# A two-layer streaming encoder on one core: weight low parts on VectorE, x1 and x3 held whole, z's gain moved to its rows, later turns and norm

## The chip, the core and the metric

The kernel runs on one core of a Trainium2 chip. The metric is device time in microseconds (us). Before the change the kernel took 2825.17 us, the median of 3 runs (2823.48 to 2830.65). A program of the core sends work to five engines, each with its own queue served in order: TensorE (PE; weight loads are shown apart as PEld), VectorE (DVE), ScalarE (ACT), GpSimd (POOL) and SyncE (SP), which issues the transfers.

## The reference, cut to what matters

Sequence 2048, width 1024, 16 heads of 64, all in float32. Layer 0 is a causal pooling mixer, layer 1 is stick-breaking attention; each is followed by a gated embedding.

```python
def rms_norm(x, g):
    return x * rsqrt(mean(x * x, axis=-1) + EPS) * g

def pool_mixer(h, w_in, w_group, scale, w_out):
    u, z = split(h @ w_in, 2)
    # four channel groups: trailing means over 2, 4, 8, 16 frames, minus the frame
    mixed = einsum('bsgc,gcd->bsgd', pooled(u), w_group) * scale
    return (mixed * silu(z)) @ w_out

# layer 0
x = x + pool_mixer(rms_norm(x, a_norm), a_w_in, a_w_group, a_scale, a_w_out)
x = x + (p[0] @ ple_w[0]) * sigmoid(x @ ple_gate_w[0])
# layer 1
k, v = split(rms_norm(x, kv_norm) @ w_kv, 2)
q, z = split(rms_norm(x, b_norm) @ b_w_in, 2)
k, q = rms_norm(heads(k), k_norm), rms_norm(heads(q), b_q_norm)
# strictly causal, beta = sigmoid(q.k / 8), blocks of 128 queries
o = sum over s < t of beta[t,s] * prod(1 - beta[t,j], s < j < t) * v[s]
x = x + (o * silu(z)) @ b_w_out
x = x + (p[1] @ ple_w[1]) * sigmoid(x @ ple_gate_w[1])
```

In the kernel's words x1 is the stream after the mixer's residual, x2 the stream after layer 0, x3 the stream after the attention's residual.

## The kernel before

**Layout.** The stream is held transposed: 8 tiles of 128 channels, in 4 chunks of 512 tokens, so a tile is 128x512. Every float32 operand of a product is split in two tiles, a high part (`F32R`, a cast of the value, on ScalarE) and a low part (value minus high part), and a product is three matmuls: high by high, high by low, low by high. `split` (L188, L189) does this for activations, with the low part on the engine that its caller names; `put_split` does it for weights.

**Weights.** `plan` lists all weight units in the order in which they are used; `pump` loads them ahead into 9 buffers (`wpair`), and `take` and `give_back` move along that list. A unit's raw tile lies in `io`, a ring of 4 buffers that other loads use too. For weights without a gain (a norm's factor per input channel), ScalarE casts the high part (L208, kept in program order), and a counter `lo` decides who makes the low part (L210): in the first stage (boot) VectorE, then two of three on GpSimd and the third on VectorE. For weights with a gain, ScalarE multiplies by it (L214) and VectorE does the low part (L215), twice for a unit, once for each of its halves.

**Stages.** The program is one long list of steps, one for each matmul, and what is to happen some steps later is put off by `after`, `late` and `store`.

1. Opening (solo: no attention runs). Chunk 0's mixer and `gated_part(0)`, chunk 1's mixer and `gated_part(1)`. Side work is drawn in steps: `prep` loads, splits and squares the next chunk's x; `mixtures` makes combined weights for the job (in `mx` tiles); `prefill` scales chunk 0's x2 rows for it.
2. `pair_part(0, 1)`, the first *job*: v, k and q of two chunks by a scheme of seven products (p1 to p7) on half-width blocks in place of eight. The PSUM tiles are `total` and `own`. Row sets: p1 and p2 come from `prefill`, the others from `build`, whose first four steps make p5, p7, p3 and p6 and the next four p4. It ends with `reload`, which loads the first chunk's x2 rows, scales them by the norm (L844) and splits them on GpSimd, for z.
3. Attention for the queries of chunks 0 and 1 (48 slots, each a head and a chunk of keys), with `beside_first` drawn beside it: z of chunks 0 and 1, chunk 2's mixer and gate, chunk 3's mixer. VectorE runs the scans of the attention (L1126) and the low parts of `at` (L1146) there.
4. `middle`: `gated_part(3)` and `pair_part(2, 3)`, the second job.
5. Attention for chunks 2 and 3 (112 slots), beside z of chunks 2 and 3 and the output part `post` of chunks 0 to 2; then `post(3)` alone.

**x1 and x3.** `out_steps` adds the residual into the loaded tile `xr` (in `io`), splits the sum into a pair and keeps only the pair. `gate_steps` needs the sum again, and rebuilds it on GpSimd as `xj`, high plus low (L702, 64 times).

**Norms and turns.** `norm2` puts two tasks in a list, `lag`: the sum of squares over channels (`pst<-ones,acc`, after 24 steps) and the broadcast of the factors (`pst<-ident,r`, after 48 steps, giving `rb2`, whose tile is `rby`). For k and q, `keyed` normalises per head (L751) and puts four turns (`finish`, `pst<-ident,qs`) in the list 44 steps later: TensorE turns the tile, ScalarE copies it, GpSimd makes the low part (`hl`, L765), SyncE stores. `timed` takes one task at a time, at least 9 steps apart, as they fall due. Before each job `settled_lag` runs all tasks that are left at once, and `pair_part` runs `build`'s first four steps ahead of the first product:

```python
        side = build(c1)
        for _ in range(4):
            next(side)
        back = reload(c0)
        for n, _ in enumerate(job(c0, c1)):
            if n >= 120 and n % 10 == 0:
                next(side, None)
            if n >= total - 58 and n % 6 == 0:
                next(back, None)
```

`tmp` has 6 buffers, `row` 11, `pair` 17, `pp` 8. `row` holds the squares' sum of `prep` (`acc`), two of `prep`'s last splits (`xh`, `xl`) and the raw rows of `prefill`.

## Time and profile before

The profiled execution took 2824.62 us and its span, from the first to the last instruction, is 2822.8 us. The granted clock of TensorE was 0.975 over the span.

| stage (us of the span) | length | PE | DVE | ACT | POOL | clock |
|---|---|---|---|---|---|---|
| boot, chunk 0's mixer (0 to 140) | 140 | 136.02 | 100.48 | 71.78 | 42.53 | 1.00 |
| `gated_part(0)` and around it (140 to 260) | 120 | 99.14 | 58.05 | 61.28 | 92.17 | 0.97 |
| chunk 1's mixer, `gated_part(1)` (260 to 444) | 184 | 184.00 | 91.79 | 50.59 | 90.81 | 1.00 |
| first job (444 to 726) | 282 | 254.30 | 169.92 | 147.08 | 219.91 | 0.94 |
| first attention (726 to 1405) | 679 | 651.63 | 508.43 | 393.71 | 313.77 | 0.98 |
| `gated_part(3)` (1405 to 1450) | 45 | 38.12 | 27.17 | 19.80 | 31.44 | 0.93 |
| second job (1450 to 1749) | 299 | 257.47 | 166.82 | 146.53 | 231.19 | 0.91 |
| second attention (1749 to 2718) | 969 | 950.39 | 857.58 | 571.89 | 134.73 | 0.99 |
| `post(3)` (2718 to 2823) | 105 | 100.07 | 23.09 | 14.49 | 18.90 | 1.00 |

How to read it: the columns are busy times in us, the last is the clock that TensorE was granted. The difference between length and PE is what TensorE waited in that stage; it is largest in the first gated stage and in the two jobs, where GpSimd is at its fullest. Busy matmuls are not all at full speed: a clock below 1 means that some of them ran slower.

### The profile page before, as it was taken

What the parts mean: (1) busy time and instruction counts of PE and PEld (TensorE: products, weight loads), DVE (VectorE), ACT (ScalarE), POOL (GpSimd) and SP (SyncE); (2) the same over time, 40 slices, a digit from 0 to 9 for tenths busy, and PEclk for the clock granted to TensorE, in tenths of its full rate; (3) what the DMA queues carried; (4) which work ended last, traced back from release to release, by engine and by line L of the source; (5) the groups of instructions that cost most, each with busy time, mean ns of one, the idle gap of its engine ahead of it and who ended that gap; (6) DMA issues with size and microseconds to landing.
All of it is one profiled execution on the core that took longest, in us unless ns stands there. A gap on an engine that the chain in (4) does not pass through costs nothing.

```text
span 2822.8 us, 38660 instructions
## 1 busy us (share of the span) xinstructions
PE 2671.1 (95%) x13118; PEld 2216.6 (79%) x13118; DVE 2003.3 (71%) x2523; ACT 1477.2 (52%) x2922; POOL 1175.4 (42%) x889
## 2 busy tenths in 40 slices
PE   9988997999799998999989997999999999999999
PEld 7866886878588887888867775888888878887887
DVE  6744736465767877788574545888999888899942
ACT  5453233465676546555444564666655655555531
POOL 1468455787654426642466788100111011111111
PEclk9999998999899999999989998999999999999999
DMA  7898544856899765766448676775665556556454
GB/s 256 313 385 311 203 164 131 285 174 207 297 382 317 266 233 193 280 220 239 146 130 246 202 216 198 245 243 180 205 216 179 182 175 222 183 170 223 158 197 162
DMA packets 315362, 630.77 MB, mean 223 GB/s; under 512 B 47646, under 2 KB 80414, under 8 KB 315164
## 3 DMA queue, kind: packets, MB, share of 16 engines
q1 hardware_dynamic: 314588, 627.51, 66.6%
q8 instruction: 104, 1.70, 0.3%
q10 hardware_dynamic: 576, 0.79, 0.1%
q14 instruction: 94, 0.77, 0.1%
HBM read 463.03 MB, written 165.15 MB: 223 GB/s over the span
## 4 chain that ended last, share of the span: by engine, by line
PE 40%; DVE 9%; POOL 5%; DMA 3%; issue 3%; ACT 2%; SPq 0%; POOLq 0%; ACTq 0%; DVEq 0%
PE psd L51 19%; PE pso L51 7%; PE psl L51 6%; PE psa L55 6%; DVE pp L1126 3%; DVE at L1146 2%; PE own L51 1%; POOL wpair L210 1%; PE total L51 1%; POOL xs L189 1%; DMA wraw<-in_gate_a_dram 1%; POOL rq L181 1%; DVE sg L713 1%; POOL hl L765 1%; DMA xw<-x2d 0%
## 5 line engine op out<-in xcount | busy, mean ns | idle before, releaser
L1126 DVE TENSOR_TENSOR_SCAN pp<-pp,floor 128x512 f32<-128x512 f32 (+3 forms) x640 | 748.4, 1206 | 8.1 <-ACT pp L1122 8.0
L51 PE MATMUL psd<-x,wpair 128*128 128x512 f32 x2304 | 575.6, 395 | 28.8 <-POOL wpair L210 10.1
L51 PEld LDWEIGHTS psd<-x,wpair 128*128 128x128 f32 x2304 | 432.3, 190 | 126.3 <-POOL wpair L210 13.1
L1144 ACT CAST at<-psa 128x512 fp32r<-128x512 f32 (+3 forms) x640 | 303.5, 526 | 394.9 <-PE psa L55 393.4
L1146 DVE TENSOR_TENSOR at<-psa,at 128x512 fp32r<-128x512 f32 (+3 forms) x640 | 359.8, 601 | 139.4 <-ACT at L1144 137.8
L51 PE MATMUL pso<-at,vv 128*128 128x512 f32 (+3 forms) x1280 | 322.6, 369 | 29.5 <-DVE at L1146 23.9
L1122 ACT ACTIVATE pp<-psl 128x512 f32<-128x512 f32 (+3 forms) x640 | 312.3, 548 | 10.5 <-PE psl L51 9.9
L51 PE MATMUL psd<-xp,wpair 128*128 128x512 f32 x1248 | 303.4, 392 | 0.4 <-DVE wpair L215 0.2
L51 PEld LDWEIGHTS pso<-at,vv 128*128 128x128 f32 x1280 | 230.1, 189 | 93.5 <-DVE at L1146 42.9
L51 PE MATMUL total<-wpair,xs 128*128 128x512 f32 x1152 | 289.4, 408 | 11.8 <-POOL wpair L210 8.8
L55 PE MATMUL psa<-ident,pp 128*128 128x128 f32 x2176 | 293.7, 275 | 0.0
L55 PEld LDWEIGHTS psa<-ident,pp 128*128 128x128 f32 x2176 | 254.4, 141 | 28.1 <-issue 0.4
L51 PEld LDWEIGHTS total<-wpair,xs 128*128 128x128 f32 x1152 | 223.0, 197 | 62.0 <-POOL wpair L210 11.2
L51 PEld LDWEIGHTS psd<-xp,wpair 128*128 128x128 f32 x1248 | 231.8, 188 | 50.6 <-DVE wpair L215 1.3
L51 PE MATMUL psl<-kk,qa 128*128 128x512 f32 (+3 forms) x640 | 259.3, 410 | 0.0
L1169 POOL TENSOR_TENSOR os<-os,zt 128x512 f32<-128x512 f32 x32 | 52.1, 1629 | 488.4 <-ACT os L1168 482.8
L51 PE MATMUL psl<-kk,qb 128*128 128x512 f32 (+3 forms) x640 | 234.8, 367 | 3.4 <-ACT qb L1089 3.4
L51 PE MATMUL own<-wpair,xs 128*128 128x512 f32 x864 | 212.7, 403 | 19.4 <-ACT wpair L208 10.2
L210 POOL TENSOR_TENSOR wpair<-wraw,wpair 128x512 fp32r<-128x512 f32 x128 | 180.7, 1420 | 93.6 <-ACT wpair L208 82.8
L51 PEld LDWEIGHTS own<-wpair,xs 128*128 128x128 f32 x864 | 165.4, 194 | 57.2 <-POOL wpair L210 11.4
L702 POOL TENSOR_TENSOR xj<-x 128x512 f32<-128x512 f32 x64 | 105.5, 1653 | 202.5 <-DMA out_dram<-sg 100.9
L51 PE MATMUL psd<-og,wpair 128*128 128x512 f32 x744 | 184.5, 390 | 0.0
(144 smaller groups left out, 4042.7 us busy)
## 6 DMA issues: line engine op xcount, KB each, us to landing
wpair<-once SPq DMA_DIRECT2D x288, 512.0 KB, 4.5
kk<-kd SPq DMA_DIRECT2D x160, 256.0 KB, 3.4
vv<-vd SPq DMA_DIRECT2D x160, 256.0 KB, 3.4
once<-wpair SPq DMA_DIRECT2D x48, 512.0 KB, 6.1
wpair<-wf SPq DMA_DIRECT2D x48, 512.0 KB, 5.7
xw<-x2d SPq DMA_DIRECT2D x72, 256.0 KB, 4.5
once<-kp SPq DMA_DIRECT2D x36, 512.0 KB, 4.9
wraw<-in_gate_a_dram SPq DMA_DIRECT2D x64, 256.0 KB, 3.2
```

The costliest lines, as they stand in the source:

```text
L51: return held_in_order(nc.tensor.matmul(*a, **k))
L55: return held_in_order(nc.tensor.transpose(*a, **k))
L181: G.tensor_tensor(out=out_ap, in0=ms, in1=neghalf[:, 0:w], op=ALU.pow)
L189: low = lambda: lo.tensor_tensor(out=half_of(pr, 1), in0=src, in1=f(half_of(pr, 0)), op=ALU.subtract)
L210: (G if state["lo"] % 3 and not state["boot"] else V).tensor_tensor(out=pr[:, 1], in0=raw, in1=f(pr[:, 0]), op=ALU.subtract)
L702: G.tensor_tensor(out=xj, in0=f(x1[o][:, 0]), in1=f(x1[o][:, 1]), op=ALU.add)
L713: V.tensor_tensor(out=sg, in0=sg, in1=xj, op=ALU.add)
L1122: A.activation(out=pp[:, r0:], in_=ps[:, :w], func=AF.Sigmoid, scale=-1.0)
L1126: V.tensor_tensor_scan(out=pp[:, r0:][:, ::-1], data0=pp[:, r0:][:, ::-1], data1=least, initial=1.0 if st["diag"] else st["carry"][j], op0 ...
L1144: A.copy(out=at[:, 0, cs], in_=pt[:, cs])
L1146: return lambda: V.tensor_tensor(out=at[:, 1, cs], in0=pt[:, cs], in1=f(at[:, 0, cs]), op=ALU.subtract)
L1169: G.tensor_tensor(out=os, in0=os, in1=zt, op=ALU.mult)
```

## The change

- `put_split`: the low part of a weight without gain is on VectorE while no attention runs, and beside attention for every second weight; the others stay on GpSimd.
- `plan_z`: the weights of z are loaded without gain, so they are split by the line above; `reload` gets the gain `g_b` and multiplies it into the rows in the same pass as the norm's factors. Its raw rows now lie in `tmp` in place of `io`.
- `out_steps` can write the sum to a tile of its own in `row` (`x1`) and keep it; `gate_steps` then uses it, and nothing is rebuilt. This is done for chunks 0 and 2 of layer 0 and for all four chunks of layer 1: 48 of 64 rebuilds go. `prep` needs one `row` pair less, and takes a pair of `act` in its place.
- The turns of k and q come 60 steps after their rows in place of 44, the norm's sums after 30 in place of 24.
- `settled_lag` goes: the tasks left over fall due inside the job, and `build`'s first four steps run at the job's first step at which `rb2` is there.

```diff
@@ -207,7 +207,7 @@
         if gain is None:
             held_split(A.copy(out=pr[:, 0], in_=raw))
             state["lo"] += 1
-            (G if state["lo"] % 3 and not state["boot"] else V).tensor_tensor(out=pr[:, 1], in0=raw, in1=f(pr[:, 0]), op=ALU.subtract)
+            (V if state["solo"] or state["lo"] % 2 else G).tensor_tensor(out=pr[:, 1], in0=raw, in1=f(pr[:, 0]), op=ALU.subtract)
             return
         for i, kt in enumerate(kts):
             g = gain[:, kt : kt + 1]
@@ -311,7 +311,7 @@
 
     def plan_z():
         for b in range(4):
-            plan_block("zb", b_w_z, b, g_b, True)
+            plan_block("zb", b_w_z, b, None, True)
 
     plan_a(0)
     first_chunk = len(plan)
@@ -527,7 +527,7 @@
         for o in range(KT):
             xin = io("xin")
             nc.sync.dma_start(out=xin, in_=x[o * P : (o + 1) * P, s * W5 : (s + 1) * W5])
-            pr = pair("xp") if o < 6 else (row("xh", F32R), row("xl", F32R))
+            pr = pair("xp") if o < 7 else (row("xh", F32R), row("xl", F32R))
             split(pr, xin, G)
             ck["x"].append(pr)
             gather_squares(ck, "acc1", o, xin)
@@ -639,7 +639,7 @@
 
 
 
-    def out_steps(acts, residual, ahead=lambda: None):
+    def out_steps(acts, residual, ahead=lambda: None, whole=None):
         res, requested = [], deque()
 
         def request(o):
@@ -665,9 +665,13 @@
                 request(2 * b + k + 2)
                 if (b, k) == (2, 1):
                     ahead()
-                V.tensor_tensor(out=xr, in0=ps, in1=xr, op=ALU.add)
+                x1 = xr
+                if whole is not None:
+                    x1 = row("x1")
+                    whole.append(x1)
+                V.tensor_tensor(out=x1, in0=ps, in1=xr, op=ALU.add)
                 pr = pair("x1")
-                split(pr, xr, V if k else G, 7)
+                split(pr, x1, V if k else G, 7)
                 res.append(pr)
         return res
 
@@ -688,7 +692,7 @@
             ple.append(pr)
         return ple
 
-    def gate_steps(x1, ple, put, ahead=lambda: None):
+    def gate_steps(x1, ple, put, ahead=lambda: None, whole=None):
         for b in range(4):
             us, ul = take(4), take(1)
             if b == 1:
@@ -698,8 +702,11 @@
                 yield from product2(pss, us, x1)
             for k in range(2):
                 o = b + 4 * k
-                xj = tmp("xj")
-                G.tensor_tensor(out=xj, in0=f(x1[o][:, 0]), in1=f(x1[o][:, 1]), op=ALU.add)
+                if whole is None:
+                    xj = tmp("xj")
+                    G.tensor_tensor(out=xj, in0=f(x1[o][:, 0]), in1=f(x1[o][:, 1]), op=ALU.add)
+                else:
+                    xj = whole[o]
                 if pss:
                     ps = pss[k]
                 else:
@@ -771,7 +778,7 @@
                 after(20, lambda: marks.add((s, b)))
 
         for m in range(4):
-            lag.append((time["now"] + 44, lambda m=m: finish(m)))
+            lag.append((time["now"] + 60, lambda m=m: finish(m)))
 
     def every(gen, n, side):
         i = 0
@@ -799,7 +806,7 @@
         def spread():
             ck["rb2"] = bcast(ck["r2"], "y")
 
-        lag.append((time["now"] + 24, total))
+        lag.append((time["now"] + 30, total))
         lag.append((time["now"] + 48, spread))
 
     def gate_z(s, acts):
@@ -838,10 +845,18 @@
         make = ppt if n < 7 else qryt if n < 9 else keyt if n < 10 else valt
         return make("xs", F32R), make("xs", F32R)
 
-    def scaled(s, kt, get):
+    def scaled(s, kt, get, gain=None):
         raw = get("xw")
         nc.sync.dma_start(out=raw, in_=x2d[s][kt])
-        return raw, lambda: V.tensor_tensor(out=raw, in0=raw, in1=chunk[s]["rb2"], op=ALU.mult)
+
+        def scale():
+            rb = chunk[s]["rb2"]
+            if gain is None:
+                V.tensor_tensor(out=raw, in0=raw, in1=rb, op=ALU.mult)
+            else:
+                V.scalar_tensor_tensor(out=raw, in0=raw, scalar=gain[:, kt : kt + 1], in1=rb, op0=ALU.mult, op1=ALU.mult)
+
+        return raw, scale
 
     def prefill(s):
         sets["raw"], sets["p1"], sets["p2"] = [], [], []
@@ -961,13 +976,17 @@
     def reload(s):
         prs = chunk[s].setdefault("x2", [])
         for kt in range(KT):
-            raw, scale = scaled(s, kt, io)
+            raw, scale = scaled(s, kt, tmp, g_b)
             yield
             scale()
             pr = pair("x2")
             split(pr, raw, G)
             prs.append(pr)
 
+    def whole(ck, wanted):
+        ck["whole"] = [] if wanted else None
+        return ck["whole"]
+
     def mixed_part(s, side=(), every_n=40):
         ck = chunk[s]
         side = iter(side)
@@ -975,7 +994,7 @@
         def body():
             yield from mixer(s)
             ck["x1"] = yield from out_steps(ck["m"], lambda o: x[o * P : (o + 1) * P, s * W5 : (s + 1) * W5],
-                                            lambda: load_ple(0, s))
+                                            lambda: load_ple(0, s), whole(ck, s % 2 == 0))
 
         yield from every(body(), every_n, side)
         for _ in side:
@@ -983,24 +1002,21 @@
 
     def gated_part(s, side, every_n):
         ple = split_ple(0, s)
-        yield from every(gate_steps(chunk[s]["x1"], ple, put_x2(s)), every_n, side)
+        yield from every(gate_steps(chunk[s]["x1"], ple, put_x2(s), whole=chunk[s]["whole"]), every_n, side)
         for _ in side:
             pass
         norm2(s)
-
-    def settled_lag():
-        while lag:
-            lag.pop(0)[1]()
 
     def pair_part(c0, c1):
         pass_time(12)
         state["hold"] = True
         total = len(KINDS) * len(PRODUCTS) * 48
         side = build(c1)
-        for _ in range(4):
-            next(side)
         back = reload(c0)
         for n, _ in enumerate(job(c0, c1)):
+            if "raw" in sets and "rb2" in chunk[c1]:
+                for _ in range(4):
+                    next(side)
             if n >= 120 and n % 10 == 0:
                 next(side, None)
             if n >= total - 58 and n % 6 == 0:
@@ -1022,18 +1038,17 @@
 
     def post(c):
         load_heads(c, KT)
-        x3 = yield from out_steps(heads[c], lambda o: x2d[c][o], lambda: load_ple(1, c))
+        x3 = yield from out_steps(heads[c], lambda o: x2d[c][o], lambda: load_ple(1, c), whole(chunk[c], True))
         ple = split_ple(1, c)
         ahead = (lambda: load_heads(c + 1, 6)) if c + 2 < NSUB else lambda: None
         yield from gate_steps(x3, ple, lambda o, t: store(
-            14, out=out[o * P : (o + 1) * P, c * W5 : (c + 1) * W5], in_=t), ahead)
+            14, out=out[o * P : (o + 1) * P, c * W5 : (c + 1) * W5], in_=t), ahead, chunk[c]["whole"])
 
     def opening():
         yield from mixed_part(0)
         yield from gated_part(0, prep(1), 22)
         yield from mixed_part(1, mixtures(), 42)
         yield from gated_part(1, prefill(0), 26)
-        settled_lag()
         yield from pair_part(0, 1)
 
     def beside_first():
@@ -1051,7 +1066,6 @@
 
     def middle():
         yield from gated_part(3, prefill(2), 26)
-        settled_lag()
         yield from pair_part(2, 3)
 
     def beside_second():
```

Three places show how the order of instructions moves. First TensorE, from the last embedding product of `gated_part(1)` into the first job (`ple` is the embedding's operand, `acc` the squares' sum, `r` the norm's factors, `xs` the job's rows). Before:

```order
L51 MATMUL psd<-ple,wpair 128x512 x6
L51 MATMUL pst<-ones,acc 128x1 x4
L55 MATMUL pst<-ident,r 128x128 x4
L51 MATMUL total<-wpair,xs 128x512 x48
L51 MATMUL own<-wpair,xs 128x512 x96
```

And now:

```order
L51 MATMUL psd<-ple,wpair 128x512 x6
L51 MATMUL total<-wpair,xs 128x512 x18
L51 MATMUL pst<-ones,acc 128x1 x4
L51 MATMUL total<-wpair,xs 128x512 x18
L55 MATMUL pst<-ident,r 128x128 x4
L51 MATMUL total<-wpair,xs 128x512 x12
L51 MATMUL own<-wpair,xs 128x512 x96
```

The two norm tasks stood between the gate's last product and the job; now the job's first product p1 (`total`) starts, and they lie 18 and 36 matmuls into it.

Second GpSimd in `gated_part(0)` (`mx` are the combined weights of `mixtures`, `xp` the next chunk's x, `acc` its squares' sum; `x_1774` and the like are x1 pairs). Before:

```order
L210 TENSOR_TENSOR wpair<-wraw,wpair 128x512
L904 TENSOR_TENSOR mx<-mx 128x512
L210 TENSOR_TENSOR wpair<-wraw,wpair 128x512 x2
L189 TENSOR_TENSOR xp<-xin,xp 128x512
L702 TENSOR_TENSOR xj<-x_1774 128x512
L702 TENSOR_TENSOR xj<-x_1908 128x512
L189 TENSOR_TENSOR xp<-xin,xp 128x512
L441 TENSOR_TENSOR acc<-acc,sq 128x512
L901 TENSOR_TENSOR mx<-mx 128x512
L702 TENSOR_TENSOR xj<-x_1782 128x512
```

And now:

```order
L189 TENSOR_TENSOR xp<-xin,xp 128x512 x2
L441 TENSOR_TENSOR acc<-acc,sq 128x512
L916 TENSOR_TENSOR mx<-mx 128x512
L441 TENSOR_TENSOR acc<-acc,sq 128x512
L917 TENSOR_TENSOR mx<-mx 128x512
L918 TENSOR_TENSOR mx<-mx 128x512
L919 TENSOR_TENSOR mx<-mx 128x512
L189 TENSOR_TENSOR xp<-xin,xp 128x512
```

The low parts of weights (L210) and the rebuilt `xj` (L702) are gone.

Third the end of the first job. On TensorE, from p4 of q (`total`) to the first product of z (`psd<-x_`, in its operand the reloaded x2), with the turns of q (`pst<-ident,qs`) between. Before:

```order
L51 MATMUL total<-wpair,xs 128x512 x44
L55 MATMUL pst<-ident,qs 128x128 x4
L51 MATMUL total<-wpair,xs 128x512 x9
L55 MATMUL pst<-ident,qs 128x128 x4
L51 MATMUL total<-wpair,xs 128x512 x9
L55 MATMUL pst<-ident,qs 128x128 x4
L51 MATMUL total<-wpair,xs 128x512 x9
L55 MATMUL pst<-ident,qs 128x128 x4
L51 MATMUL total<-wpair,xs 128x512 x21
L55 MATMUL pst<-ident,qs 128x128 x4
L51 MATMUL total<-wpair,xs 128x512 x4
L51 MATMUL psd<-x_6522,wpair 128x512 x3
```

And now:

```order
L51 MATMUL total<-wpair,xs 128x512 x60
L55 MATMUL pst<-ident,qs 128x128 x4
L51 MATMUL total<-wpair,xs 128x512 x9
L55 MATMUL pst<-ident,qs 128x128 x4
L51 MATMUL total<-wpair,xs 128x512 x9
L55 MATMUL pst<-ident,qs 128x128 x4
L51 MATMUL total<-wpair,xs 128x512 x9
L55 MATMUL pst<-ident,qs 128x128 x4
L51 MATMUL total<-wpair,xs 128x512 x9
L51 MATMUL psd<-x_6490,wpair 128x512 x3
```

The turns stood 9 matmuls apart from the last part of p4 on; each now comes 16 matmuls later, and the last group's turns lie within z's product.

On VectorE in the same place (L1126 and, renumbered, L1140 are the first scans of the attention, `xw` the rows of `reload`, `zr` the first results of z, L215 and L210 the low parts of weights). Before:

```order
L844 TENSOR_TENSOR xw<-xw,rby 128x512 x2
L215 SCALAR_TENSOR_TENSOR wpair<-wraw,gains,wpair 128x256 x4
L1126 SCALAR_TENSOR_TENSOR pp<-pp,floor 128x384
L1126 SCALAR_TENSOR_TENSOR pp<-pp,floor 128x512
L215 SCALAR_TENSOR_TENSOR wpair<-wraw,gains,wpair 128x256 x2
L844 TENSOR_TENSOR xw<-xw,rby 128x512
L215 SCALAR_TENSOR_TENSOR wpair<-wraw,gains,wpair 128x256
L844 TENSOR_TENSOR xw<-xw,rby 128x512
L215 SCALAR_TENSOR_TENSOR wpair<-wraw,gains,wpair 128x256
L810 TENSOR_TENSOR zr<-psd,sg 128x512 x3
```

And now:

```order
L210 TENSOR_TENSOR wpair<-wraw,wpair 128x512
L758 TENSOR_TENSOR qs<-qs,rq 128x512
L210 TENSOR_TENSOR wpair<-wraw,wpair 128x512 x2
L758 TENSOR_TENSOR qs<-qs,rq 128x512 x2
L1140 SCALAR_TENSOR_TENSOR pp<-pp,floor 128x128
L1140 SCALAR_TENSOR_TENSOR pp<-pp,floor 128x256
L817 TENSOR_TENSOR zr<-psd,sg 128x512 x2
L210 TENSOR_TENSOR wpair<-wraw,wpair 128x512
L857 SCALAR_TENSOR_TENSOR xw<-xw,gains,rby 128x512
L210 TENSOR_TENSOR wpair<-wraw,wpair 128x512
```

Two scalings of rows and eight gained low parts stood between the first scans and `zr`; now most of the rows' scalings are ahead of the last `qs`, and only scans stand right before `zr`.

## The prediction

> **What bounds the kernel now.** I read the page's table of engines first, then the view of who waited for whom, for TensorE alone, then the same view and the timeline stretch by stretch.
>
> ```profile
> PE 2671.1 (95%) x13118; PEld 2216.6 (79%) x13118; DVE 2003.3 (71%) x2523; ACT 1477.2 (52%) x2922; POOL 1175.4 (42%) x889
> ```
> ```profile
> PE pst L55 <- DVE qs L751: 32.7, 6, 10.7
> PE pso L51 <- DVE at L1146: 23.9, 24, 3.9
> PE psd L51 <- POOL wpair L210: 12.9, 7, 3.0
> PE own L51 <- ACT wpair L208: 10.2, 2, 5.9
> PE psd L51 <- DVE zr L810: 9.9, 1, 9.9
> PE own L51 <- POOL wpair L210: 9.2, 3, 6.0
> PE total L51 <- POOL wpair L210: 8.8, 3, 4.0
> ```
>
> TensorE is the bound: 2671.1 of 2822.8 us, with the same 13118 matmuls before and after. So the change can win only from the 151.7 us in which it stands still, and from slow matmuls behind a long wait. The second price shows here (start, duration, then the idle time before the row in brackets):
>
> ```profile
> 1721.21 0.48 PE L55 MATMUL pst<-ident,qs 128*128 128x128 f32 x1 [7.78 <-DVE qs L751]
> 1721.34 4.19 PE L51 MATMUL total<-wpair,xs 128*128 128x512 f32 x9
> 1725.33 1.05 PE L55 MATMUL pst<-ident,qs 128*128 128x128 f32 x4
> 1726.03 2.79 PE L51 MATMUL total<-wpair,xs 128*128 128x512 f32 x9
> 1728.66 0.60 PE L55 MATMUL pst<-ident,qs 128*128 128x128 f32 x4
> 1729.02 2.32 PE L51 MATMUL total<-wpair,xs 128*128 128x512 f32 x9
> ```
>
> Nine matmuls take 2.32 us at full speed, but 4.19 and then 2.79 after a wait of 7.78: a cold restart costs 1.87 + 0.47 = 2.3 us beside the wait. The Trainium skill (TensorE: Matmul & The Clock Gate, Part 1) puts it as half rate for about 3.4 us after at least 3.4 us of idling, an estimated 1.7 us for each such wait and none for a shorter one; three long waits removed would be about 5 by it, where term 6 has 7.
>
> **Term 1, the first gated stage (140 to 260 us).** The window's busy times, in the order PE, PEld, DVE, ACT, POOL; then the same lows (L210) by engine, DVE before POOL; then two of them on VectorE:
>
> ```profile
> 197.00:260.00 63.00, 49.87 (x198) 39.01 (x199) 34.97 (x25) 32.94 (x56) 61.85 (x44) 0.95 0.87 300
> ```
> ```profile
> 140.00:260.00 120.00, 11.40 (x9) 26.13 (x19) 0.97 0.95 343
> ```
> ```profile
> 188.88 0.69 DVE L210 TENSOR_TENSOR wpair<-wraw,wpair 128x512 fp32r<-128x512 f32 x1 [1.53 <-ACT wpair L208]
> ...
> 209.08 1.78 DVE L210 TENSOR_TENSOR wpair<-wraw,wpair 128x512 fp32r<-128x512 f32 x1
> ```
>
> GpSimd is full (61.85 of 63), VectorE is not (34.97). The change takes from GpSimd 19 lows (26.13 us) and the 8 rebuilt x1 tiles, and gives VectorE the lows at 0.69 us alone or 1.78 beside GpSimd's work. VectorE keeps room: even with all 19 of them at 1.2, between the two rows, it would be busy for 58 of 63. All seven waits for GpSimd's lows (12.9 us) sit here. I leave 3 of them for VectorE's own queue (mixtures stand in it) and take 2 from earlier freed input buffers, x1 no longer lying in them until its split is done: **-12**, between -18 (the casts' waits go too) and +5 (the lows now queue behind mixtures).
>
> The Trainium skill (SBUF — State Buffer, "Who interferes with whom") speaks against this move: a VectorE operation with two SBUF inputs and a GpSimd operation that reads SBUF exclude each other. The rows 0.69 and 1.78 agree. If every moved low paid it on TensorE's path, terms 1 and 3 together would be about -4 in place of -19; I don't go by that, since a moved low also takes away one of the GpSimd operations that it could meet.
>
> **Term 2, the start of the two jobs.**
>
> ```profile
> 448.03 1.87 PE L51 MATMUL pst<-ones,acc 128*128 128x1 f32 x8 [3.71 <-POOL acc L441]
> 451.53 1.11 PE L55 MATMUL pst<-ident,r 128*128 128x128 f32 x4 [1.64 <-POOL r L181]
> 452.30 13.69 PE L51 MATMUL total<-wpair,xs 128*128 128x512 f32 x48
> 465.82 11.74 PE L51 MATMUL own<-wpair,xs 128*128 128x512 f32 x51
> 481.85 1.22 PE L51 MATMUL own<-wpair,xs 128*128 128x512 f32 x2 [4.29 <-ACT wpair L208]
> 489.13 12.69 PE L51 MATMUL own<-wpair,xs 128*128 128x512 f32 x43 [6.05 <-POOL wpair L210]
> ```
> ```profile
> 452.68 0.59 ACT L418 COPY rby<-pst 128x512 f32<-128x512 f32 x1 [2.59 <-PE pst L55]
> ...
> 481.19 1.14 ACT L208 CAST wpair<-wraw 128x512 fp32r<-128x512 f32 x2
> ```
>
> Products p1 and p2 now start at once (448.03 - 3.71 = 444.3), with the norm between them, so the 3.71 + 1.64 vanish. But nothing before p5 counts: p5 needs the build, which needs the norm, and the weights' casts stand in ScalarE's queue behind the build's casts (481.19, that is 27.9 us after the norm's copy ended at 453.3). The order puts the norm's broadcast behind 36 matmuls: 444.3 + 36 x 0.23 (11.74 / 51) + 1.87 = 454.5, 3.0 later than 451.53; and it puts the build's last loads behind three stores of qs on SP's queue, for which I add 1. The second p5 weight, whose cast ended at 481.8, is then cast at 485.8, and its low follows on VectorE (0.69) instead of GpSimd: 486.5, where TensorE got it at 489.13. It arrives there at 444.3 + 99 x 0.23 + 3 = 470 and **waits some 16 us in one piece**, where it waited 4.29 + 6.05. So the early start is given back, and only the shorter low gains: 2.6, say 3, for each job, **-6**, between -16 (the last loads aren't delayed, and the build runs faster with GpSimd freer) and +6.
>
> **Term 3, later weights inside the jobs.** The waits of `total` for GpSimd's lows are 8.8 us; on VectorE, whose queue holds only short evacuations there, they nearly go: **-7**, between -9 and 0.
>
> **Term 4, the end of the jobs.** The view of waits for 640 to 760, then for 1640 to 1760, then GpSimd in 692 to 738 and its last split of x2:
>
> ```profile
> PE psd L51 <- DVE zr L810: 9.9, 1, 9.9
> PE pst L55 <- DVE qs L751: 8.2, 2, 6.6
> PE psd L51 <- POOL x L189: 2.1, 3, 1.1
> ```
> ```profile
> PE pst L55 <- DVE qs L751: 24.4, 4, 10.7
> ```
> ```profile
> 692.00:738.00 46.00, 42.64 (x35) 0.93 0.67 217
> ```
> ```profile
> 735.03 3.17 POOL L189 TENSOR_TENSOR x<-xw,x 128x512 fp32r<-128x512 f32 x2
> ```
>
> Turns of q come 16 matmuls (3.7 us) later, those of the group before the last only inside the z product, so the two long waits for qs (6.6 and 10.7) go and the others shrink. What is late next is x2, which GpSimd splits, full until 738.2. It is spared one hl and two lows of about 1.4 before that, so x2 is ready 4.2 earlier, while TensorE comes 8.2 earlier: it waits 2.1 + 8.2 - 4.2, about 6. The 9.9 for zr goes: on VectorE the scalings of the next chunk's rows, with their loads, no longer stand between the scans and zr; I leave 2. First job: 8.2 + 2.1 + 9.9 = 20.2 becomes 8, **-12** (-18 to +5). Second: 24.4, where x2 was in time, becomes 6 + 3, **-15** (-22 to 0).
>
> **Term 5, second attention.** Rebuilt x3 tiles slow VectorE there (GpSimd's row, then VectorE's):
>
> ```profile
> 2314.38 3.84 POOL L702 TENSOR_TENSOR xj<-x 128x512 f32<-128x512 f32 x2
> ```
> ```profile
> 2311.35 4.15 DVE L1126 TENSOR_TENSOR_SCAN pp<-pp,floor 128x512 f32<-128x512 f32 x2
> ...
> 2319.89 2.48 DVE L1126 TENSOR_TENSOR_SCAN pp<-pp,floor 128x512 f32<-128x512 f32 x2
> ```
>
> The same two scans take 4.15 or 2.48. 24 such rebuilds go from this stretch. Of the 23.9 us that TensorE waits for `at`, I take **-5** (-10 to 0).
>
> **Term 6, cold restarts.** Three of the four long waits of term 4 leave without a new long one: 3 x 2.3, **-7** (-14 to 0). At p5 one restart stays.
>
> **At nothing:** z's gain in the rows (one cast and one low a unit in place of two and two; the rows' scaling gets one more factor in the same pass), hidden behind TensorE's 95%; x1 and x3 in rows of their own, which were free. In the first attention VectorE gets half the lows in place of a third, and z's, without their gained form; GpSimd loses 8 rebuilds. I take 0, between -11 and +15: z's casts are now held in order on ScalarE, and a late load would hold the casts of `at` queued behind them, for which TensorE waits.
>
> **Sum.** -12 - 6 - 7 - 12 - 15 - 5 - 7 = -64. The profiled execution took 2824.62 us (0.6 below the median of 2825.17): **2761**. Terms off by half to both sides give its own range, 2739 to 2783.
>
> **Rivals.**
> - *More is freed.* x2 is ready at both job ends (-14) and the first attention's waits go (-11): 2736. For it: GpSimd loses whole operations just there. Against: 42.64 of 46 us on GpSimd.
> - *The waits change place.* z waits for x2 as long as for qs before (term 4 falls to -5, term 6 to 0): 2761 + 22 + 7 = 2790. For it: the same full GpSimd makes both.
> - *It doesn't do what it says.* Turns and norm come later, and each wait moves with them: only the lows' terms 1, 3 and 5 are left, -24: 2801.
> - *Slower: the lows are caught in VectorE's queue.* It is served in order and stands still for loads of rows (idle time behind the second bar):
>
> ```profile
> L844 DVE TENSOR_TENSOR xw<-xw,rby 128x512 f32<-128x512 f32 x72 | 68.7, 983 | 60.6 <-DMA xw<-x2d 40.3 <-ACT rby L418 20.2
> ```
>
>   If the 40.3 us reach the weights queued behind and so TensorE, while the 30.9 that it waited for GpSimd's lows come back as well and five restarts with them: 2761 + 40 + 31 + 12 = 2844. It decides above 64 us of new waits. Against: most of these loads stand where no weight is due within the next product.
>
> **How the numbers follow.** Forecast 0.56, more freed 0.12, waits change place 0.18, doesn't do it 0.07, slower 0.07. The range for 8 in 10 goes from 2733 to 2805, taking in all but the slower case and the tails. About 0.3% (8 us) can be told from no change: faster 0.90 (the first four cases, less tails), same 0.05, slower 0.05.
>
> **What would show it.** Right: no wait for lows of GpSimd in the jobs; one wait of 12 to 18 us at the third matmul group of `own`; no wait of `pst` over 4 us for qs, and `psd` waiting for GpSimd's x2 in its place; clean scans beside the last stages. Wrong: a `pst` wait as long as before, a new wait of `pso` for ScalarE while z is split, or lows on VectorE with waits for loads ahead of them.

## The result and the profile after

The changed kernel takes 2781.3 us, the median of 4 runs (2780.76 to 2782.63); the kernel before took 2827.15 us beside it (median of 4, 2823.48 to 2830.65). The ratio is 0.9839, with a 95% interval of 0.9822 to 0.9856. That is 45.9 us faster by the medians and 42.0 by the two profiled spans (2822.8 and 2780.8 us). The forecast was 2761 us with a range of 2733 to 2805: the direction and the range held, and a third of the expected gain is missing.

The page's table of engines, for the kernel after:

```profile
PE 2659.5 (96%) x13118; PEld 2210.2 (79%) x13118; DVE 2051.4 (74%) x2623; ACT 1469.6 (53%) x2906; POOL 943.0 (34%) x725
```

GpSimd lost 232 us of work and VectorE took 48. Of the 42.0 us, 11.6 are faster matmuls (2671.1 to 2659.5 us of PE), and 30.4 are waits of TensorE that went. Who waited for whom, for TensorE, after (total us, times, longest):

```profile
PE own L51 <- ACT wpair L208: 38.2, 2, 19.2
PE psd L51 <- POOL x L189: 15.5, 8, 4.0
PE pso L51 <- DVE at L1160: 15.3, 16, 2.5
PE psl L51 <- ACT qb L1103: 8.1, 5, 3.6
PE psd L51 <- ACT wpair L208: 7.0, 3, 4.3
```

Of the old list, the waits for qs, for zr and for GpSimd's lows are gone, and those for `at` went from 23.9 to 15.3. The first two rows, 54 us for p5's weights and x2, had 21.5 before (10.2 and 9.2 for p5's weights, 2.1 for x2). To see where the time came and went, I counted TensorE's matmuls in the two timelines and compared when the n-th begins. The offset (after minus before) is good to about 1 us inside one pair of profiles. Between profiles, the boot, which is the same code in all of them, already differs by up to 3 us.

| stretch (us of before) | forecast's terms | forecast | measured |
|---|---|---|---|
| to 410, first gated stage | 1 | -12 | -8.6 |
| 410 to 522, first job's start | 2, first half | -3 | +1.5 |
| 522 to 700, in the first job | 3, part | -3 | -1.2 |
| 700 to 875, its end and the attention's start | 4, 6 | -17 | +7.7 |
| 875 to 1403, rest of the first attention | none | 0 | -6.2 |
| 1403 to 1516, second job's start | 2, second half | -3 | +1.7 |
| 1516 to 1705, in the second job | 3, part; first of the qs waits | -4 | -13.6 |
| 1705 to 1809, its end | 4, 6 | -17 | -12.7 |
| 1809 to the end | 5 | -5 | -10.6 |
| sum | | -64 | -42.0 |

The cold restarts of term 6 (-7) are put to the ends of the jobs here. The second job's long waits for qs begin ahead of 1705, so its last two rows are best read together, -26.3 against -21.

### The profile page after: what moved, and what is told of

Read it like the earlier page. It is cut to its first block, busy times and chain, and to the rows that moved or that the text cites. A ratio compares the mean times of both kernels' runs of the same rounds, so it can differ in the third digit from the quotient of the medians.

```text
span 2780.8 us, 38541 instructions
## 1 busy us (share of the span) xinstructions
PE 2659.5 (96%) x13118; PEld 2210.2 (79%) x13118; DVE 2051.4 (74%) x2623; ACT 1469.6 (53%) x2906; POOL 943.0 (34%) x725
## 4 chain that ended last, share of the span: by engine, by line
PE 67%; DVE 15%; DMA 8%; issue 3%; ACT 3%; POOL 2%; SPq 1%; DVEq 0%; ACTq 0%; POOLq 0%
PE psd L51 34%; PE pso L51 8%; PE psl L51 7%; PE psa L55 7%; PE total L51 5%; PE own L51 5%; DVE pp L1140 4%; DVE at L1160 2%; DVE wpair L210 1%; DVE us L574 1%; PE pst L55 1%; DMA xw<-x2d 1%; DMA mx<-in_w_kv_dram 1%; DMA uraw<-in_wu_t_dram 1%; DMA once<-wpair 1%
## 5 line engine op out<-in xcount | busy, mean ns | idle before, releaser
L1140 DVE TENSOR_TENSOR_SCAN pp<-pp,floor 128x512 f32<-128x512 f32 (+3 forms) x640 | 736.4, 1188 | 2.6 <-ACT pp L1136 2.5
L51 PE MATMUL psd<-x,wpair 128*128 128x512 f32 x2304 | 583.6, 399 | 23.8 <-POOL x L189 15.5
L51 PE MATMUL pso<-at,vv 128*128 128x512 f32 (+3 forms) x1280 | 319.6, 367 | 18.4 <-DVE at L1160 15.3
L51 PE MATMUL psd<-xp,wpair 128*128 128x512 f32 x1392 | 336.8, 392 | 0.3 <-DVE wpair L215 0.2
L51 PEld LDWEIGHTS psd<-xp,wpair 128*128 128x128 f32 x1392 | 259.0, 188 | 55.7 <-DVE wpair L215 1.1
L51 PE MATMUL total<-wpair,xs 128*128 128x512 f32 x1152 | 279.5, 399 | 5.0 <-DVE wpair L210 3.7
L210 DVE TENSOR_TENSOR wpair<-wraw,wpair 128x512 fp32r<-128x512 f32 x193 | 189.4, 1000 | 125.8 <-ACT wpair L208 123.2
L51 PEld LDWEIGHTS total<-wpair,xs 128*128 128x128 f32 x1152 | 217.3, 191 | 53.5 <-DVE wpair L210 5.4
L51 PE MATMUL psd<-mp,wpair 128*128 128x512 f32 x768 | 182.1, 395 | 4.3 <-ACT wpair L208 4.3
```

Of the source, the lines that this page charges most:

```text
L51: return held_in_order(nc.tensor.matmul(*a, **k))
L210: (V if state["solo"] or state["lo"] % 2 else G).tensor_tensor(out=pr[:, 1], in0=raw, in1=f(pr[:, 0]), op=ALU.subtract)
L1140: V.tensor_tensor_scan(out=pp[:, r0:][:, ::-1], data0=pp[:, r0:][:, ::-1], data1=least, initial=1.0 if st["diag"] else st["carry"][j], op0 ...
```

## The places one by one, after

**First gated stage.** The window 197 to 260 of the kernel after, in the order PE, PEld, DVE, ACT, POOL:

```profile
197.00:260.00 63.00, 57.09 (x246) 45.84 (x245) 40.94 (x39) 36.36 (x63) 49.36 (x34) 0.97 0.98 351
```

GpSimd fell from 61.85 to 49.36 of 63 us and VectorE rose from 34.97 to 40.94. The 12.9 us of waits for GpSimd's lows became 1.0 for VectorE's; 3.7 more for sigmoids (1.2 before, 4.9 now) came in their place.

**Start of the first job.** TensorE after, from the job's first matmul to p6, and one row of the kernel before, its p6:

```profile
435.31 4.35 PE L51 MATMUL total<-wpair,xs 128*128 128x512 f32 x18
...
444.61 0.60 PE L55 MATMUL pst<-ident,r 128*128 128x128 f32 x4
444.96 3.02 PE L51 MATMUL total<-wpair,xs 128*128 128x512 f32 x12
447.82 11.72 PE L51 MATMUL own<-wpair,xs 128*128 128x512 f32 x51
478.73 1.22 PE L51 MATMUL own<-wpair,xs 128*128 128x512 f32 x2 [19.18 <-ACT wpair L208]
...
483.47 11.27 PE L51 MATMUL own<-wpair,xs 128*128 128x512 f32 x40 [1.73 <-DVE wpair L210]
494.58 11.04 PE L51 MATMUL total<-wpair,xs 128*128 128x512 f32 x48
```
```profile
501.65 11.33 PE L51 MATMUL total<-wpair,xs 128*128 128x512 f32 x48
```

From the end of the gate to p6 it was 501.65 - 444.3 = 57.3 us, and it is 494.58 - 435.3 = 59.3. The early start is given back, as forecast, and 2 us more. Why p5 waits 19 us and not 16, in ScalarE's queue and in VectorE's after, and two rows of SyncE's view of waits (440 to 480):

```profile
445.24 0.59 ACT L418 COPY rby<-pst 128x512 f32<-128x512 f32 x1 [4.59 <-PE pst L55]
...
478.06 2.17 ACT L208 CAST wpair<-wraw 128x512 fp32r<-128x512 f32 x4
```
```profile
453.09 0.69 DVE L926 TENSOR_TENSOR qs<-total,qs 128x512 f32<-128x512 f32 x1
...
455.50 0.69 DVE L926 TENSOR_TENSOR qs<-total,qs 128x512 f32<-128x512 f32 x1
...
457.48 3.46 DVE L889 TENSOR_TENSOR xw<-xw 128x512 f32<-128x512 f32 x2
460.87 0.68 DVE L926 TENSOR_TENSOR qs<-total,qs 128x512 f32<-128x512 f32 x1
...
464.22 3.42 DVE L189 TENSOR_TENSOR xs<-xw,xs 128x512 fp32r<-128x512 f32 x2
...
478.71 1.33 DVE L210 TENSOR_TENSOR wpair<-wraw,wpair 128x512 fp32r<-128x512 f32 x1 [1.72 <-ACT wpair L208]
479.96 1.76 DVE L855 TENSOR_TENSOR xw<-xw,rby 128x512 f32<-128x512 f32 x1
481.65 8.52 DVE L210 TENSOR_TENSOR wpair<-wraw,wpair 128x512 fp32r<-128x512 f32 x5
```
```profile
SPq L70 <- DVE qs L926: 14.6, 2, 12.3
...
SPq L850 <- DVE xs L189: 4.0, 1, 4.0
```

The casts come 32.2 us after the norm's copy, 27.9 before. The build's last row is loaded only at 466, 20 us after the norm's copy. SyncE's queue has passed the stores of qs (L70) by then: the wait that ends last is 4.0 us for a buffer that VectorE's split (L189) frees. On VectorE the evacuations of p1 and p2 (`qs`) now stand between the build's steps, and two of these steps, additions (L889), take 3.46 us beside GpSimd's splits. With the early start the lows on VectorE bring nothing at p5: that of the second p5 weight takes 1.33 us, so TensorE gets it 44.8 us after the gate's end (480.10 - 435.3), just as long as before (489.13 - 444.3); the next weight's low stands behind the scaling of a row (L855), and TensorE waits 1.73 us more for it. The second job is the same: its gate ends 9.0 us earlier than before (1432.7), and its p6 starts 5.1 earlier.

**End of the first job.** TensorE after, the first products of z:

```profile
709.12 1.75 PE L51 MATMUL psd<-x,wpair 128*128 128x512 f32 x7
712.39 0.96 PE L51 MATMUL psd<-x,wpair 128*128 128x512 f32 x3 [1.52 <-POOL x L189]
716.22 1.65 PE L51 MATMUL psd<-x,wpair 128*128 128x512 f32 x3 [2.87 <-POOL x L189]
719.59 1.65 PE L51 MATMUL psd<-x,wpair 128*128 128x512 f32 x3 [1.72 <-POOL x L189]
725.20 8.59 PE L51 MATMUL psd<-x,wpair 128*128 128x512 f32 x28 [3.96 <-POOL x L189]
```

No wait for qs and none for zr, but four for x2, 10.1 us, with slow matmuls behind the last three of them: three take 1.65 us where seven took 1.75. From 700 to 763 us (of before) the offset goes from -8.3 to -16.3, so 8 us are won here of the 12 to 17 forecast. Then the attention's first 100 us give it all back, in waits of 0.4 to 3.6 us for qb, at and hl (13.0 us in all from 745 to 880, where the kernel before has 1.7 from 760 on), and at 875 us the offset is -0.6.

## Experiments

All are of the whole kernel, with runs of the kernel before beside them on the same chip; the ratio to those is what is compared (the changed kernel: 0.9839).

### One part undone

Lows back on the old engines:

```diff
-            (V if state["solo"] or state["lo"] % 2 else G).tensor_tensor(out=pr[:, 1], ...
+            (G if state["lo"] % 3 and not state["boot"] else V).tensor_tensor(out=pr[:, 1], ...
```

> The changed kernel with the old rule for the low parts of weights (boot: VectorE, then two of three on GpSimd). Theory (the forecast's terms 1, 3 and part of 2 come from this line): the waits for GpSimd's lows come back, about 8 us in the first gated stage and 6 to 12 in the jobs, so 2795 to 2803 us against 2781. Rival (GpSimd is freed enough by the dropped rebuilds and by z; where the lows stand does not matter): 2780 to 2786 us, and the first gated stage keeps its 8 to 9 us.

Measured: 2802.18 us, ratio 0.9905 (0.9887 to 0.9922). The first gated stage gained 4 to 5 us less, the waits for GpSimd's lows were back (8.9, 8.4 and 6.3 us for psd, own and total), and the first job lost 6 more. The theory holds: this line is worth about 20 us (20.9 by the medians, 18.7 by the ratios).

Gain of z back in the weights:

```diff
-            plan_block("zb", b_w_z, b, None, True)
+            plan_block("zb", b_w_z, b, g_b, True)
...
-            raw, scale = scaled(s, kt, tmp, g_b)
+            raw, scale = scaled(s, kt, io)
```

> The changed kernel with z's weights gained again and the reloaded rows scaled by the norm alone, in io buffers. Theory: the 9.9 us for zr at the first job's end come back, and the new waits of psl for qb in the first 150 us of the attention (6.2 us beside 2.2 before) go, since z's casts are no longer held in order on ScalarE: 2778 to 2790 us, the offset to before about -8 at 750 us and no longer shrinking after it. Rival (the qb waits come from the order of the whole attention's start, not from z): the 9.9 come back and the qb waits stay, 2788 to 2795 us.

Measured: 2780.58 us, ratio 0.9828 (0.9809 to 0.9848), no difference that can be told. Its view of waits has

```profile
PE psl L51 <- ACT qb L1103: 7.2, 4, 3.6
...
PE pst L55 <- DVE qs L758: 3.8, 1, 3.8
...
PE psd L51 <- DVE zr L817: 1.9, 1, 1.9
```

Both theory and rival are wrong on zr: TensorE waits 1.9 us for it and not 9.9, so moving the gain isn't what removed most of that wait. The qb waits stay, so z's casts don't make them.

Sums rebuilt:

```diff
-                                            lambda: load_ple(0, s), whole(ck, s % 2 == 0))
+                                            lambda: load_ple(0, s), whole(ck, False))
...
-        x3 = ... lambda: load_ple(1, c), whole(chunk[c], True))
+        x3 = ... lambda: load_ple(1, c), whole(chunk[c], False))
...
-            pr = pair("xp") if o < 7 else (row("xh", F32R), row("xl", F32R))
+            pr = pair("xp") if o < 6 else (row("xh", F32R), row("xl", F32R))
```

> The changed kernel without the kept sums: every x1 and x3 is rebuilt on GpSimd again, and prep has its old pairs. Theory (forecast's term 5): the 8 to 10 us that the second attention gained (offset -31 at 1800 us, -42 at 2700) go, and 2 to 4 in the first gated stage: 2790 to 2796 us. Rival (the gain there comes from the lows on VectorE, which leave GpSimd free, or from z): within 4 us of 2781.

Measured: 2814.43 us, ratio 0.9953 (0.9939 to 0.9968). The direction is the theory's, the size is more than twice as large: 33 us by the medians. The profiled execution took only 2806.52 us, the least of the six, so the offsets place 24 of them: 12 us are lost in the second attention, 6 in the first gated stage, and 5 to 6 from the first job's end through the first attention.

Turns 44 steps after their rows:

```diff
-            lag.append((time["now"] + 60, lambda m=m: finish(m)))
+            lag.append((time["now"] + 44, lambda m=m: finish(m)))
```

> The changed kernel with the turns of k and q 44 steps after their rows again. Theory (forecast's term 4): pst waits for qs at the ends of both jobs again, 6 to 10 us each with a cold restart, and z waits less for x2 in exchange: first job's end about +2, second's +10, so 2788 to 2796 us. Rival (waits only change place between qs and x2): 2779 to 2784 us.

Measured: 2785.55 us, ratio 0.9844 (0.9827 to 0.9861): nothing that can be told. At the ends of the jobs pst waits for qs 1.5 us (first) and not at all (second). So the later turns by themselves didn't remove the long waits for qs.

Norm and build's first steps ahead of the job:

```diff
-        lag.append((time["now"] + 30, total))
+        lag.append((time["now"] + 24, total))
...
+        while lag:
+            lag.pop(0)[1]()
+        for _ in range(4):
+            next(side)
         back = reload(c0)
         for n, _ in enumerate(job(c0, c1)):
-            if "raw" in sets and "rb2" in chunk[c1]:
-                for _ in range(4):
-                    next(side)
```

> The changed kernel with the norm's sums after 24 steps, the list of tasks emptied ahead of each job and build's first four steps ahead of the first product, as before. Theory (forecast's term 2: the early start is given back at p5): the two waits of about 19 us in one piece become 4 to 6 and 6 each again, the 5 us ahead of each job come back, and the time changes by less than 4 us: 2777 to 2785 us. Rival (the early start is a gain that only p5 hides, since the build runs earlier too): 2788 to 2795 us. For the qb waits of the first attention, which stayed in each of the four runs before: if the order of tasks makes them they go here and the offset stays at about -10 after 770 us; if transfers do, which fill 0.9 to 1.03 of the DMA engines from 740 to 880 us in every kernel, they stay.

Measured: 2772.24 us, ratio 0.98 (0.9783 to 0.9817), some 10 us **faster** than with this part of the change; neither theory nor rival had that. The waits for qb stay, 8.2 us. ScalarE, VectorE and TensorE of this kernel in the first job:

```profile
442.23 0.59 ACT L418 COPY rby<-pst 128x512 f32<-128x512 f32 x1 [2.59 <-PE pst L55]
...
469.65 2.18 ACT L208 CAST wpair<-wraw 128x512 fp32r<-128x512 f32 x4
```
```profile
452.49 1.89 DVE L889 TENSOR_TENSOR xw<-xw 128x512 f32<-128x512 f32 x3
...
454.90 3.48 DVE L189 TENSOR_TENSOR xs<-xw,xs 128x512 fp32r<-128x512 f32 x2
...
460.01 0.68 DVE L926 TENSOR_TENSOR qs<-total,qs 128x512 f32<-128x512 f32 x1
```
```profile
432.61 1.52 PE L51 MATMUL psd<-ple,wpair 128*128 128x512 f32 x6
...
470.32 13.65 PE L51 MATMUL own<-wpair,xs 128*128 128x512 f32 x45 [4.10 <-ACT wpair L208]
483.80 1.52 PE L51 MATMUL total<-wpair,xs 128*128 128x512 f32 x6
```

The build's additions (three take 1.89 us) and this split come before the first evacuation: the split starts 12 us after the norm's copy ended (442.8), against 18, and the casts come 26.8 after it, against 32.2. From the gate's end (434.1) to p6 it is 49.7 us, against 59.3 with the early start and 57.3 before. So each job's start had 7.6 us to win from the lows on VectorE (the second wait of p5, 6.05, is gone), and the norm inside the job spends 9.6. The run with the lows alone, below, wins 7.5 there too. Not all of this reaches the end: by the offsets this kernel is 19 us ahead of the change at the second job's p6, 14 at 1705 us and 11.5 at the end.

### One part alone

Lows on VectorE, nothing else changed:

> The kernel before with only the new rule for the low parts of weights without gain (z's keep their gain here). Theory (this line carries terms 1 and 3 by itself): 12 to 22 us less than before, most of it in the first gated stage and the jobs. Rival (it pays only together with the dropped rebuilds, since undoing either cost 21 and 33 us, more than the whole gain of 46 leaves for them): less than 8 us.

Measured: 2806.07 us, ratio 0.9914 (0.9899 to 0.9929), 23.5 us less than before, a little more than the theory had, and about what undoing the line costs in the changed kernel. The line pays by itself. The long waits for zr and qs are still there in this kernel:

```profile
PE pst L55 <- DVE qs L751: 26.6, 6, 11.6
...
PE psd L51 <- DVE zr L810: 9.7, 1, 9.7
```

### Contention or waiting for the sum

The sums are kept and used, and GpSimd makes them all the same into tiles that nobody reads:

```diff
                 else:
+                    G.tensor_tensor(out=tmp("xj"), in0=f(x1[o][:, 0]), in1=f(x1[o][:, 1]), op=ALU.add)
                     xj = whole[o]
```

> The changed kernel, x1 and x3 kept, with GpSimd rebuilding the 48 sums all the same into tiles that nobody reads. It tells contention from waiting for the sum. Theory (the rebuilds cost by being on GpSimd: scans and low parts of VectorE beside them run slower, and GpSimd's queue in the first gated stage is longer): most of the 25 to 33 us of the run with rebuilt sums comes back, 2800 us or more, and waits of pso for VectorE's at of some 24 us. Rival (somebody waited for the sums, or for the input buffers which they hold up): within 5 us of 2781, pso's waits at 15 us.

Measured: 2808.55 us, ratio 0.9918 (0.9901 to 0.9935): 27 us by the medians, 22 by the ratios, for 48 operations whose results nobody waits for. VectorE's scans, after and with the unread sums:

```profile
L1140 DVE TENSOR_TENSOR_SCAN pp<-pp,floor 128x512 f32<-128x512 f32 (+3 forms) x640 | 736.4, 1188 | 2.6 <-ACT pp L1136 2.5
```
```profile
L1141 DVE TENSOR_TENSOR_SCAN pp<-pp,floor 128x512 f32<-128x512 f32 (+3 forms) x640 | 752.2, 1213 | 2.5 <-ACT pp L1137 2.5
```

The same 640 scans take 15.8 us more. They stand in one queue with `at`, for which TensorE waits, here from 1740 us to the end: before, after, and with the unread sums.

```profile
PE pso L51 <- DVE at L1146: 17.3, 15, 3.9
```
```profile
PE pso L51 <- DVE at L1160: 10.9, 8, 2.5
```
```profile
PE pso L51 <- DVE at L1161: 20.9, 17, 3.9
```

This settles that most of the rebuilds' cost (22 to 27 of some 33 us) comes from their running on GpSimd, with the `tmp` tiles and the pairs that they hold, and not from anybody waiting for their sums. Of the 26 us between the two profiles, 10.7 are the wait for `at` and 6.7 slower matmuls (2666.2 us of PE in place of 2659.5); the rest is spread over smaller waits.

### What is late next

p5's casts ahead of the build's:

```diff
-            if "raw" in sets and "rb2" in chunk[c1]:
+            if n == 52 and "raw" in sets:
+                for u, _ in held:
+                    settle(u)
                 for _ in range(4):
                     next(side)
```

> The changed kernel with the casts of p5's weights 52 steps into the job and build's first four steps after them, so that ScalarE does these casts ahead of the build's. Theory (p5 waits for its weights' casts only, which stand behind the build's last casts; the last row set is ready some 4 us before them): the waits of 19 us become 14 to 16, 6 to 10 us less in all: 2771 to 2776 us. Rival (the build's last row, loaded late, comes last anyway): waits as long, now for xs, 2779 to 2784 us.

Measured: 2778.53 us (2775.07 to 2781.76), ratio 0.9821 (0.9803 to 0.9838). p5's wait is 16.1 us in five pieces, now for the rows (`xs`) on VectorE and ScalarE. The offset says 4 to 5 us less per job; the runs can't tell it from no change. What the rival named, the build's late rows, is the next cause behind the casts.

x2's low parts on VectorE at the ends of the jobs:

```diff
-            split(pr, raw, G)
+            split(pr, raw, V if state["solo"] else G)
```

> The changed kernel with the low parts of the reloaded x2 on VectorE at the ends of the jobs. Theory (forecast's term 4: GpSimd's split of x2 is late next): the waits of psd for GpSimd's x2, 10.1 and 5.4 us, mostly go with the slow matmuls behind them: -8 at the first job's end and -5 at the second, 2766 to 2774 us, if the first attention doesn't take the first back; 2774 to 2779 if it does. Rival (the rows' loads or the norm's scaling are as late as GpSimd): 2779 to 2784 us.

Measured: 2771.72 us, ratio 0.9791 (0.9777 to 0.9806), 10 us faster than the change by the medians, 14 by the ratios. From 640 to 800 us

```profile
PE psd L51 <- DVE x L189: 4.5, 2, 2.7
```

stands where x2 on GpSimd made 10.1 us. GpSimd's split of x2 was late next, and 10 us or more hung on it.

Both together, and then with every second of these low parts left on GpSimd (`V if state["solo"] and kt % 2 else G`):

> The changed kernel with both edits that gained: the norm and build's first steps ahead of the job as before, and the low parts of the reloaded x2 on VectorE at the jobs' ends. Theory (two places, two queues, so the gains of 9 and 9.6 add up): 2760 to 2765 us. Rival (a later wait takes one of them back, as the first attention took some 10 us back in every kernel so far): 2767 to 2773 us.

> As the run with both edits, but only every second low part of the reloaded x2 is on VectorE at the jobs' ends, the others stay on GpSimd. Theory (GpSimd's queue and VectorE's are both short enough then, and x2's pairs come faster than with either alone): 2 to 5 us less than with all on VectorE, 2756 to 2762 us, waits of psd for x2 under 5 us in all. Rival (the rows' loads set the pace): the same as with all on VectorE within 2 us.

Measured: 2759.74 us, ratio 0.9752 (0.9737 to 0.9766), and 2758.18 us, ratio 0.9743 (0.9726 to 0.9759). The two gains add up: by the ratios 0.39% and 0.48% below the change, and 0.87% together. Sharing x2 between the engines makes no difference that can be told. The last one is the fastest kernel of this study: the change without its norm inside the job, with x2's low parts on two engines, 23 us faster than the change.

### The attention's first 100 us

In all variants above the offset rises between 773 and 875 us, by 6 us with the lows alone and by 8 to 12 in the others. Here the splitting of the output weights beside the attention begins later:

```diff
-                if count % 42 == 0 and kept:
+                if count % 42 == 21 and count > 200 and kept:
```

> The run with half of x2's low parts on VectorE, and the splitting of the output weights beside the first attention begins 231 steps into it in place of 42 (the same 36 units, at the same distance, later). In all kernels but the one before, the first 100 us of the attention gave 8 to 13 us back (offset to before from -24.5 at 773 us to -13.6 at 875 us in the run this one starts from). Theory (the stretch from 740 to 880 us is full: its transfers take 0.9 to 1.03 of the DMA engines, and the casts of these units stand in ScalarE's queue ahead of qb and at; less of that work there, less is given back): the offset at 875 us is -18 or lower and the time 2750 to 2755 us. Rival (the order of scans, rows and casts on VectorE and ScalarE makes these waits, with or without that work): the offset stays at -11 to -16, 2756 to 2760 us.

Measured: 2762.77 us, ratio 0.9768 (0.975 to 0.9786), so no gain over the run that it starts from (2758.18, 0.9743). The offset at 875 us is -20.3, as the theory had it, but the rise is still 7.7 us where it was 10.9, and by 1456 us the 6 us are lost again. What makes most of this rise is open. What the trace of the changed kernel shows is a chain of small delays, here on VectorE, then ScalarE and TensorE:

```profile
835.86 3.12 DVE L1140 TENSOR_TENSOR_SCAN pp<-pp,floor 128x384 f32<-128x384 f32 x2
839.01 1.60 DVE L1175 TENSOR_TENSOR os<-own,os 64x512 f32<-64x512 f32 x1
```
```profile
840.65 1.28 ACT L1182 ACTIVATE os<-os,en 128x128 f32<-128x128 f32 x4 [2.99 <-DVE os L1175]
```
```profile
843.81 0.33 PE L51 MATMUL psl<-kk,qb 128*128 128x128 f32 x1 [3.60 <-ACT qb L1103]
```

The same two scans take 2.06 us at 799.57, and the same addition 0.69 at 780.74: slowed by 1 us each, they hold the biases on ScalarE, and qb's copy stands behind these in its queue. The kernel before did the same work with no wait over 1.7 us there.

## Why the prediction was right, and where not

**Right.** TensorE is the bound and can win only from its waits and slow matmuls: the split of the 42 us shows it. The lows (terms 1 and 3, and the 2.6 in each job's start) were forecast at -24 and are worth 20 to 24 us in two experiments. The rule that spoke against them (the Trainium skill, SBUF — State Buffer, "Who interferes with whom"), priced as the prediction had it, would have had -4 for terms 1 and 3 in place of -19: moving a low between the two engines that exclude each other does pay here. A likely reason, which no run tests by itself, is that an operation that slowed VectorE goes with it. The unread sums, with scans slower by 15.8 us, agree with the rule itself. z's gain was costed at nothing, and undoing it changes nothing that can be told. The account closes roughly: the lows (about 20 us) and the kept sums (22 to 33) win more than the 42 to 46 measured, and the norm inside the jobs gives some 10 back.

That the total came as near as it did is in part luck. Against the table's forecasts five rows fall short by 39 us together (the first gated stage, both starts of the jobs, the middle of the first job, and its end with the attention's start), and the others win 17 more than was forecast.

**Term 2, the start of the jobs, failed.** The step has "it puts the build's last loads behind three stores of qs on SP's queue, for which I add 1": the casts came 4.3 us later against the norm, and what held the last load was a buffer that VectorE freed late, with the evacuations between the build's steps. The norm's copy itself came 1.5 us later against the gate's end than before, where 3.0 were taken for its broadcast. The "2.6, say 3" of the shorter low failed with it: it was priced at 0.69 us, took 1.33, and the weight came no sooner than before. The sum, -6, is +3.2 in the table. The larger miss is in what it was measured against: without the norm inside the job the lows alone would have won 7.6 at the first start.

**Term 4, the end of the first job, failed.** The step has "it waits 2.1 + 8.2 - 4.2, about 6" for x2: TensorE waited 10.1, with slow matmuls after three of the four pieces that the step had at nothing. And the 8 us that were won there by 763 us were lost in the attention's first 100 us, where the prediction had 0, between -11 and +15. So the rival in which the waits change place came true at this one place (10.1 us for x2 where qs had 8.2), and not at the second job's end. There x2 made only 5.4:

```profile
PE psd L51 <- POOL x L189: 5.4, 4, 1.9
PE pso L51 <- DVE at L1160: 2.5, 1, 2.5
PE pst L55 <- DVE at L1160: 1.8, 2, 1.5
```

**Term 4's reasons don't stand alone.** The forecast put the end of the qs waits down to the later turns, and that of zr to the scalings of rows that leave VectorE. With turns at 44 the qs waits stay away; with z's gain back the wait for zr is 1.9, and one of 3.8 for qs returns at the second job's end; with the lows back neither returns; with the lows alone both are there. Several edits together remove them, and no run here says which of them suffice.

**Term 5 was mis-sized by half.** -5 was taken of a bound of -10; the stretch gave -10.6, and undoing the kept sums loses 12 us there. The mechanism (VectorE's scans slowed by GpSimd) is confirmed by the unread sums. The rebuilds' cost in the first attention, some 3 to 4 us after 875 in the two runs that have them back, was not in the sum, and may be part of the -6.2 there.

**Term 6** was -7; all matmuls together are 11.6 us faster, and the restarts behind qs and zr aren't told apart from the other slow matmuls in that.

## What to carry to other kernels

Work that nobody waits for can still cost time, if it runs on GpSimd beside a VectorE that a bound engine waits for: count operations there, and test with an unread copy of one. A bound engine that starts a stage earlier wins only if what the stage needs in its middle starts earlier too; look in each queue at what the early start puts ahead of that, and which buffers come free later for it. Where a long wait goes, price the next one behind it in pieces, with the slow matmuls that follow each piece.

## What was not expected of the hardware

Waits of 1.5 to 4 us in a row, with 3 matmuls between them, slowed the matmuls as one long wait does. The granted clock was 1.00 from 712.4 to 715.8 us and 0.50 from 715.8 to 729.4: three took 1.65 us (0.55 each) after a wait of 2.87 and again after one of 1.72, and the 28 behind the last took 8.59 us, where 0.23 each would make 6.4. The rule in the table of the Trainium skill (TensorE: Matmul & The Clock Gate, Part 1), which asks for about 3.4 us of idling, would have had full speed after each of these but the last, so here the measurement decides against it.
